# A decoder layer on one core: values ahead of the next scores, one scale on GpSimd, wider splits and sums, reciprocals in pieces

## The chip, the cores and the metric

The kernel runs on one core of a Trainium2 chip. The core has TensorE (PE, with its weight loads shown as PEld), VectorE (DVE), ScalarE (ACT), GpSimd (POOL) and SyncE (SP), which issues most of the transfers. The metric is the device time of one execution in microseconds. All times here are from the kernel's own runs and from one profiled execution of it.

## The reference

One decoder layer over 512 tokens of width 1024, all in float32: a sparse attention (NSA, 8 heads of 64, 2 key/value heads) and a gated linear attention (GLA, 4 heads) side by side, then a cross attention to 256 memory tokens and a gated feed-forward layer with a short convolution. Cut to what the change touches:

```python
for l in range(DEPTH):                                   # DEPTH = 1
    h = rms_norm(x, ln_mix_g)
    q_a, kv_a, gate_a, q_b, k_b, v_b, r_b, alpha_b, merge = split(h @ w_in)
    # NSA: for each block of queries three attentions (compressed, selected, window)
    #   s = q k - slope * distance; p = masked_softmax(s); o = p v
    #   out = gate0 * o_cmp + gate1 * o_slc + gate2 * o_win
    # GLA: b = cumsum(log_sigmoid(a_low @ w_alpha2 + b_alpha) / 16)  in chunks of 64 tokens
    #   q_d = q exp(b); k_d = k exp(-b); k_s = k exp(b_last - b)
    #   o = causal(q_d k_d^T) v + q_d state;  o = o * rsqrt(mean(o*o) + eps) * norm_g * silu(r)
    mix = sigmoid(m_nsa) * (o_nsa @ w_branch_nsa) + sigmoid(m_gla) * (o_gla @ w_branch_gla)
    x = x + mix @ w_out
    x = x + memory_cross_attention(rms_norm(x, ln_x_g), rms_norm(mem, ln_mem_g))
    x = x + conv_ffn(rms_norm(x, ln_ffn_g))              # (gelu(conv(u)) * g) @ w_down
return rms_norm(x, ln_final_g)
```

With 8 blocks of 64 tokens and 8 to select, the selected attention sees every earlier key.

## The kernel before

Activations are kept transposed, 128 features by 512 tokens a tile. Each float32 operand x of a product is split into h (rounded, by ACT) and l = x - h (by DVE), and a product is three matmuls: `mm3` (L160 to L162). Weights come in 141 blocks of 128x1024 from one array; `convert` (L140 on ACT, L141 on DVE) splits each block as it arrives. `split` (L165 ACT, L166 DVE) does the same for activations; it is a helper, so its instructions are told apart by their tiles.

The stages follow each other as proj, nsa, gla, mem/mix/mkv/wout, xat, xo, up/down. The NSA stage is a loop over 2 key/value heads (kv) and 4 query blocks of 128 tokens (i):

- `nsa_scores(kv, i)` makes scores for four heads g (L597 to L613 on PE), adds the position bias and takes maxima on DVE (L603, L615), scales the maxima (L622), takes exponentials with sums on ACT (L631), makes the coefficients on DVE (L634 reciprocal, L635), and multiplies the probabilities in place: the selected part `ss[g]` on DVE for g = 0, 1, 2 (L639) and on ACT for g = 3 (L641), the window part `sw[g]` on ACT for even g (L643) and on GpSimd for odd g (L645), the compressed part on GpSimd (L646). `ss` is 128x128(i+1), `sw` at most 128x384.
- `nsa_values(kv, i, ...)` transposes the probabilities of all four heads on PE (L669), splits them (tiles pth, ptl, pc), and accumulates the products with the values (L663) in one bank; then it adds two halves (L688) and splits the output into the tiles ON, two 128x128 pieces per block.
- between them, `fill` puts in work of the GLA projections ("fill" tiles: dense products of 24 matmuls, and `gla_decay` with its cumulative sums at L450).

The program states the operations in the order of the Python text. At build time each operation is put into the queue of its engine: of those that are then estimated to be ready, the one that stands earlier in the program goes first. Each engine runs its queue strictly in that fixed order. So matmuls of "fill" stand among those of the scores in the PE queue, and a later operation of the program stands behind an earlier one on its engine where both are ready.

Buffers are pools of equal tiles by tag: 43 of "g" (128x512), 16 of "s", 4 of "pair" (128x2x512). In `rsqrt` (L227, L228) ACT takes the root and DVE the reciprocal of the whole tile.

Of the kernel before, what the change touches and what calls it, by code (L numbers as in the profile page):

```python
# [10 lines left out]
F32R = mybir.dt.float32r  # L11
U32 = mybir.dt.uint32
AF = mybir.ActivationFunctionType
ALU = mybir.AluOpType
AX = mybir.AxisListType

P = 128
T = 512
# [17 lines left out]
def _layout(items):  # L36
# [14 lines left out]

CO, CO_COLS = _layout([
    ("ident", 128), ("ones", 128), ("slc", 512), ("win", 384), ("cmp", 124),
    ("chunk", 128), ("nslope", 24), ("slope", 8), ("qscale", 4), ("valid", 1), ("eps", 1),
])


# [1 line left out]
def layer_kernel(ctx: ExitStack, tc: tile.TileContext, xT, memT, W, small, const, gfin, out, out_t, order):  # L59
    nc = tc.nc  # L60
# [5 lines left out]
    def sb(shape, dtype, tag, bufs):  # L66
        uid[0] += 1
        return pool.tile(shape, dtype, name=f"{stage[0]}_{tag}_{uid[0]}", tag=tag, bufs=bufs)

    GB, SB, TB = 43, 16, 6  # L70

    def g_(dtype=F32):
        return sb([P, T], dtype, "g", GB)


    def pair():
        return sb([P, 2, T], F32R, "pair", 4)

    def s_(dtype=F32):
        return sb([P, T], dtype, "s", SB)  # L80
# [23 lines left out]
    def C(name):  # L104
        a, b = CO[name]
        return cst[:, a:b]
# [57 lines left out]
    def split(h, l, src):  # L164
        nc.scalar.activation(h, src, AF.Copy)  # L165
        nc.vector.tensor_sub(l, src, h.bitcast(F32))  # L166
# [58 lines left out]

    def rsqrt(dst, src, scale, refine=False):
        nc.scalar.activation(dst, src, AF.Sqrt, scale=scale, bias=C("eps"))  # L227
        nc.vector.reciprocal(dst, dst)  # L228
        if refine:
            v = sb([P, 4], F32, "newton", 2)[:, :dst.shape[-1]] if dst.shape[-1] <= 4 else t_()[:, :dst.shape[-1]]  # L230
            nc.vector.scalar_tensor_tensor(v, src, EPS / scale, dst, op0=ALU.add, op1=ALU.mult)
            nc.vector.scalar_tensor_tensor(v, v, -0.5 * scale, dst, op0=ALU.mult, op1=ALU.mult)
            nc.vector.scalar_tensor_tensor(dst, v, 1.5, dst, op0=ALU.add, op1=ALU.mult)
# [187 lines left out]
    def gla_decay():  # L421
        alT = bank("pt")
        for t in range(4):
            nc.tensor.transpose(alT[0:16, t * P:(t + 1) * P], alpha[t], C("ident"))
        als, wa = t_(F32R), sb([P, 256], F32R, "walpha", 1)
        nc.gpsimd.memset(als.bitcast(F32), 0.0)
        nc.gpsimd.memset(wa.bitcast(F32), 0.0)
        nc.scalar.activation(wa[0:16], S("walpha")[0:16], AF.Copy)
        nc.scalar.activation(wa[32:48], S("walpha")[0:16], AF.Copy)
        nc.vector.tensor_sub(wa[64:80], S("walpha")[0:16], wa[0:16].bitcast(F32))  # L430
        split(als[0:16], als[32:48], alT[0:16])
        nc.scalar.activation(als[64:80], alT[0:16], AF.Copy)
        zs = []
        az = sb([P, 2, T], F32, "raw", 3)
        for m in range(2):
            ps = bank("pt")
            nc.tensor.matmul(ps, wa[:, m * P:(m + 1) * P], als, start=True, stop=True)
            z = t_()
            nc.scalar.activation(z, ps, AF.Identity, bias=S("b_alpha")[:, m:m + 1])
            nc.scalar.activation(az[:, m], ps, AF.Abs, bias=S("b_alpha")[:, m:m + 1])  # L440
            zs.append(z)
        nc.scalar.activation(az, az, AF.Exp, scale=-1.0)
        nc.scalar.activation(az, az, AF.Ln, bias=1.0)
        for m in range(2):
            z = zs[m]
            nc.vector.scalar_tensor_tensor(z, z, 0.0, az[:, m], op0=ALU.min, op1=ALU.subtract)
            cs = g_()
            for c in range(8):
                v = slice(c * 64, c * 64 + 64)
                nc.vector.tensor_tensor_scan(cs[:, v], C("ones")[:, 0:64], z[:, v], 0.0, op0=ALU.mult, op1=ALU.add)  # L450
            cum[m] = cs


# [108 lines left out]
    fillers.append(gla_k(1))  # L562


    ON = [None] * 4

    def nsa_scores(kv, i):
        n = P * (i + 1)
# [66 lines left out]
        nc.vector.tensor_mul(cf, cf, gates[i][:, kv * 12:(kv + 1) * 12].rearrange("p (g b) -> p b g", b=3))  # L635
        for g in range(4):
            a, b = ss[g][:, :n], sw[g][:, :nw]
            if g < 3:
                nc.vector.tensor_scalar(a, a, cf[:, 1, g:g + 1], None, op0=ALU.mult)  # L639
            else:  # L640
                nc.scalar.activation(a, a, AF.Copy, scale=cf[:, 1, g:g + 1])  # L641
            if g % 2 == 0:
                nc.scalar.activation(b, b, AF.Copy, scale=cf[:, 2, g:g + 1])  # L643
            else:
                nc.gpsimd.tensor_scalar(b, b, cf[:, 2, g:g + 1], None, op0=ALU.mult)  # L645
# [2 lines left out]

    def nsa_values(kv, i, j0, ss, sw, cm):
        if i == 0:  # L650
            for a in range(2):
                ON[kv * 2 + a] = (g_(F32R), g_(F32R))
        qs = slice(i * P, (i + 1) * P)
        jobs = [([ss[g][:, kt * P:(kt + 1) * P] for g in range(4)], V2[kt][:, kv, :]) for kt in range(i + 1)]
        for kt in range(j0, i + 1):
            jobs.append(([sw[g][:, (kt - j0) * P:(kt - j0 + 1) * P] for g in range(4)], V2[kt][:, 2 + kv, :]))
        jobs.append(([cm[:, g] for g in range(4)], VC[:, kv, :]))
        po = bank("o")
        last = len(jobs) - 1

        def product(j, v, *parts):
            for x in parts:
                nc.tensor.matmul(po, v, x, start=j == 0 and x is parts[0], stop=j == last and x is parts[-1])  # L663

        ready = None
        for j, (srcs, v) in enumerate(jobs):
            pt = bank("pt")
            for g in range(4):
                nc.tensor.transpose(pt[:, g * P:(g + 1) * P], srcs[g], C("ident"))  # L669
            if j < last:  # L670
                h, l = sb([P, T], F32R, "pth", 2), sb([P, T], F32R, "ptl", 2)
                split(h, l, pt)
                parts = (h, l)
            else:
                x = PC[i % 2]
                split(x[0:32], x[32:64], pt[0:32])
                parts = (x,)
            if ready is not None:
                product(*ready)
            ready = (j, v) + parts  # L680
        product(*ready)
        bot = t_()
        nc.scalar.activation(bot[0:64], po[64:128], AF.Copy)
        of = t_()[:, 0:2 * P].rearrange("p (a q) -> p a q", a=2)
        pv = po.rearrange("p (a b q) -> p a b q", a=2, b=2)
        bv = bot.rearrange("p (a b q) -> p a b q", a=2, b=2)
        for b in range(2):
            nc.vector.tensor_add(of[b * 64:(b + 1) * 64], pv[0:64, :, b, :], bv[0:64, :, b, :])  # L688
        for a in range(2):
            h, l = ON[kv * 2 + a]  # L690
            split(h[:, qs], l[:, qs], of[:, a])

    stage[0] = "nsa"
    prev = None
    for kv in range(2):
        for i in range(4):
            cur = nsa_scores(kv, i)
            if prev is not None:
                nsa_values(*prev)
            prev = cur  # L700
            fill(NSA_FILL[kv * 4 + i])
    nsa_values(*prev)

# [201 lines left out]
    for n in range(0, 8, 2):  # L905
        th = [merge(C_MG, n, t_), merge(C_MG, n + 1, t_)]
        for j in range(2):
            ps = branch("w_branch_gla", OG, n + j)
            nc.vector.scalar_tensor_tensor(th[j], th[j], 1.0, ps, op0=ALU.add, op1=ALU.mult)
            nc.gpsimd.tensor_tensor(th[j], pm[n + j], th[j], op=ALU.add)  # L910
            if n < 4:
                x = pair()
                h, l = x[:, 0], x[:, 1]
            else:
                h, l = g_(F32R), g_(F32R)
            split(h, l, th[j])
            mix.append((h, l))

# [75 lines left out]
    def xat_values(hd, prs):  # L994
        po = bank("o")
        vs = slice(hd * P, (hd + 1) * P)
        for kt in range(2):
            pt = bank("pt")
            for i in range(4):
                c = (i % 2) * MEM + kt * P  # L1000
                nc.tensor.transpose(pt[:, i * P:(i + 1) * P], prs[i // 2][:, c:c + P], C("ident"))
            h, l = sb([P, T], F32R, "pth", 2), sb([P, T], F32R, "ptl", 2)
            split(h, l, pt)
            mm3(po, (XV[kt][0][:, vs], XV[kt][1][:, vs]), (h, l), kt == 0, kt == 1)
        h, l = g_(F32R), g_(F32R)
        split(h, l, po)
        xo[hd] = (h, l)

# [49 lines left out]
    def up(fs):  # L1058
# [14 lines left out]
        for f in fs:  # L1073
# [11 lines left out]
            gm = s_()  # L1085
            nc.vector.tensor_mul(gm, pg2, rstd)
            nc.gpsimd.tensor_tensor(gm, gm, cv, op=ALU.mult)  # L1087
            if f - fs[0] < 4:
                x = pair()
                h, l = x[:, 0], x[:, 1]  # L1090
            else:
                h, l = g_(F32R), g_(F32R)
            split(h, l, gm)
            act.append((h, l))
        return act
# [163 lines left out]
def _const(np):  # L1259
    z = np.zeros((P, CO_COLS), np.float32)  # L1260

    def put(name, a):
        a0, a1 = CO[name]
        z[:, a0:a1] = a
# [52 lines left out]
```

## Time and profile before

| what | value |
|---|---|
| median of 3 runs | 867.87 us (867.67 to 869.98) |
| profiled execution, its own time | 867.91 us |
| its span | 866.1 us, so 1.8 us lie around it |
| PE busy | 848.0 us, 98% of the span |
| DVE busy | 565.4 us, 65% |
| ACT busy | 425.6 us, 49% |
| POOL busy | 177.7 us, 21% |

In the rows, a group of instructions is named by line, engine, operation and tiles (out<-in), and a bracket at the end of a row of the timeline gives the engine's idle time before it and what ended that.

### The profile page before, as it was taken

How to read it: one execution, taken by the hardware profiler on the slowest of the kernel's cores; microseconds unless marked ns; L12 is line 12 of the kernel's file. 1: busy time of each engine (PE TensorE's matmuls, PEld its weight loads, DVE VectorE, ACT ScalarE, POOL GpSimd, SP SyncE). 2: the span in 40 equal slices, each digit the busy share in tenths (PEclk: the TensorE clock that was granted, in tenths of full speed). 3: DMA queues.
4: the chain of work that ended last, by engine and by line, in shares of the span. 5: the costliest groups of instructions: out<-in, count | busy, mean ns of one | idle time of the engine just before them, and what ended most of it. 6: DMA issues, size and time to landing. Idle time of an engine off the chain costs nothing.

```text
span 866.1 us, 11096 instructions
## 1 busy us (share of the span) xinstructions
PE 848.0 (98%) x4172; PEld 705.9 (81%) x4172; DVE 565.4 (65%) x923; ACT 425.6 (49%) x742; POOL 177.7 (21%) x157
## 2 busy tenths in 40 slices
PE   9999999999999999999999999999999999999997
PEld 6988767777887888898888888888888888888996
DVE  7576897998979576464487669666433456556324
ACT  7466868788544455354455535433311233334311
POOL 2373343331000023202200312111100121211121
PEclk9999999999999999999999999999999999999999
DMA  8332212002121242244341132222222222223302
GB/s 291 117 128 98 73 50 73 26 1 97 50 73 55 92 146 98 97 149 145 127 140 49 50 121 98 98 98 97 98 98 97 98 98 96 99 92 104 122 25 98
DMA packets 26407, 83.58 MB, mean 97 GB/s; under 512 B 3056, under 2 KB 5104, under 8 KB 26352
## 3 DMA queue, kind: packets, MB, share of 16 engines
q1 hardware_dynamic: 26064, 82.58, 28.1%
q8 instruction: 33, 0.54, 0.2%
q10 hardware_dynamic: 288, 0.28, 0.1%
q14 instruction: 22, 0.18, 0.1%
HBM read 80.76 MB, written 2.10 MB: 96 GB/s over the span
## 4 chain that ended last, share of the span: by engine, by line
PE 84%; DVE 7%; ACT 5%; issue 2%; POOL 1%; DVEq 0%; POOLq 0%; ACTq 0%
PE up_ps_sc L160 4%; PE up_ps_sc L161 4%; PE up_ps_sc L162 4%; PE fill_ps_acc L160 3%; PE up_ps_pt L160 3%; PE up_ps_pt L161 3%; PE up_ps_pt L162 3%; PE fill_ps_acc L161 3%; PE fill_ps_acc L162 3%; PE up_ps_acc L160 3%; PE up_ps_acc L161 3%; PE up_ps_acc L162 3%; ACT nsa_s L631 2%; PE down_ps_sc L162 2%; PE down_ps_sc L161 2%
## 5 line engine op out<-in xcount | busy, mean ns | idle before, releaser
L1087 POOL TENSOR_TENSOR up_s<-up_s,up_s 128x512 f32<-128x512 f32 x22 | 38.0, 1728 | 256.9 <-ACT up_wh L140 203.9
L140 ACT ACTIVATE up_wh<-up_raw 128x1024 fp32r<-128x1024 f32 x40 | 42.5, 1062 | 60.1 <-PE up_ps_sc L161 33.2
L141 DVE TENSOR_TENSOR up_wl<-up_raw,up_wh 128x1024 fp32r<-128x1024 f32 x40 | 61.6, 1541 | 15.5 <-ACT up_wh L140 15.3
L160 PE MATMUL up_ps_sc<-xo_g,up_wh 128*128 128x512 f32 x124 | 48.3, 389 | 0.0
L162 PE MATMUL up_ps_sc<-xo_g,up_wl 128*128 128x512 f32 x124 | 48.3, 389 | 0.0
L161 PE MATMUL up_ps_sc<-xo_g,up_wh 128*128 128x512 f32 x124 | 48.2, 389 | 0.0
L160 PE MATMUL up_ps_pt<-xo_g,up_wh 128*128 128x512 f32 x104 | 40.5, 389 | 0.0
L162 PE MATMUL up_ps_pt<-xo_g,up_wl 128*128 128x512 f32 x104 | 40.5, 389 | 0.0
L161 PE MATMUL up_ps_pt<-xo_g,up_wh 128*128 128x512 f32 x104 | 40.5, 389 | 0.0
L631 ACT ACTIVATE nsa_s<-nsa_s,nsa_nm 128x128 f32<-128x128 f32 (+3 forms) x64 | 34.2, 536 | 9.8 <-DVE nsa_nm L622 9.8
L160 PE MATMUL fill_ps_acc<-in_g,fill_wh 128*128 128x512 f32 x96 | 38.3, 399 | 0.2 <-DVE fill_t L548 0.2
L162 PE MATMUL fill_ps_acc<-in_g,fill_wl 128*128 128x512 f32 x96 | 38.1, 397 | 0.0
L161 PE MATMUL fill_ps_acc<-in_g,fill_wh 128*128 128x512 f32 x96 | 37.9, 395 | 0.0
L160 PE MATMUL up_ps_acc<-xo_g,up_wh 128*128 128x512 f32 x88 | 34.2, 389 | 0.0
L161 PE MATMUL up_ps_acc<-xo_g,up_wh 128*128 128x512 f32 x88 | 34.2, 389 | 0.0
L162 PE MATMUL up_ps_acc<-xo_g,up_wl 128*128 128x512 f32 x88 | 34.2, 389 | 0.0
L1083 ACT ACTIVATE up_s<-up_s 128x512 f32<-128x512 f32 x22 | 13.8, 632 | 40.6 <-DVE up_s L1081 40.6
L140 ACT ACTIVATE down_wh<-down_raw 128x1024 fp32r<-128x1024 f32 x9 | 9.5, 1061 | 39.4 <-PE down_ps_sc L161 17.5
L162 PEld LDWEIGHTS up_ps_sc<-xo_g,up_wl 128*128 128x128 f32 x124 | 23.3, 188 | 4.9
L160 PEld LDWEIGHTS up_ps_sc<-xo_g,up_wh 128*128 128x128 f32 x124 | 23.3, 188 | 4.8
L161 PEld LDWEIGHTS up_ps_sc<-xo_g,up_wh 128*128 128x128 f32 x124 | 23.3, 188 | 4.8
L165 ACT ACTIVATE nsa_pth<-nsa_ps_pt 128x512 fp32r<-128x512 f32 x38 | 21.8, 591 | 10.1 <-PE nsa_ps_pt L669 9.9
(975 smaller groups left out, 2687.4 us busy)
## 6 DMA issues: line engine op xcount, KB each, us to landing
up_raw<-in_w SPq DMA_DIRECT2D x44, 512.0 KB, 3.2
fill_raw<-in_w SPq DMA_DIRECT2D x20, 512.0 KB, 3.2
down_raw<-in_w SPq DMA_DIRECT2D x18, 512.0 KB, 3.3
proj_raw<-in_w SPq DMA_DIRECT2D x14, 512.0 KB, 3.8
mix_raw<-in_w SPq DMA_DIRECT2D x12, 512.0 KB, 3.2
mkv_raw<-in_w SPq DMA_DIRECT2D x8, 512.0 KB, 3.2
wout_raw<-in_w SPq DMA_DIRECT2D x8, 512.0 KB, 3.4
in_s<-in_xT SPq DMA_DIRECT2D x8, 256.0 KB, 5.5
```

The source lines that it names most:

```text
L140: nc.scalar.activation(wh[:, c], r[:, c], AF.Copy)
L141: lo.tensor_tensor(wl[:, c], r[:, c], wh[:, c].bitcast(F32), op=ALU.subtract)
L160: nc.tensor.matmul(ps, w[0], x[0], start=first, stop=False)
L161: nc.tensor.matmul(ps, w[0], x[1], start=False, stop=False)
L162: nc.tensor.matmul(ps, w[1], x[0], start=False, stop=last)
L165: nc.scalar.activation(h, src, AF.Copy)
L631: nc.scalar.activation(s[:, :w], s[:, :w], AF.Exp, scale=sl, bias=nm[:, c:c + 1], accum_out=sums[:, c:c + 1])
L1083: nc.scalar.activation(cv, cv, AF.Gelu_apprx_tanh)
L1087: nc.gpsimd.tensor_tensor(gm, gm, cv, op=ALU.mult)
```

## The change

1. In the loop of the NSA stage, the program states `nsa_values` of the block before ahead of `nsa_scores` of the block at hand, no longer behind it.
2. The selected part of head g = 1 is multiplied on GpSimd, ahead of the window part of that head, no longer on DVE.
3. The output tiles of NSA come two to a pair, and the split of a block's output is one operation on 128x2x128 on either engine, no longer two on 128x128.
4. The cumulative sums of the decay are one scan of 512 per tile, no longer eight of 64; a new constant "reset" (0 at the start of each 64, else 1) is multiplied in. The constants grow by 512 columns, 256 KB.
5. The reciprocal in `rsqrt` goes in pieces of at most 128 columns.
6. Buffers: "g" 43 to 35, "pair" 4 to 8, so split tiles of NSA's output, mix, cross attention and of 8 of the 11 activations of `up` come from pairs; a scratch for transfers shrinks from 4096 to 1024.

```diff
-    ("chunk", 128), ("nslope", 24), ("slope", 8), ("qscale", 4), ("valid", 1), ("eps", 1),
+    ("chunk", 128), ("nslope", 24), ("slope", 8), ("qscale", 4), ("valid", 1), ("eps", 1), ("reset", 512),
...
-    GB, SB, TB = 43, 16, 6
+    GB, SB, TB = 35, 16, 6
...
-        return sb([P, 2, T], F32R, "pair", 4)
+        return sb([P, 2, T], F32R, "pair", 8)
+
+    def pair_hl():
+        x = pair()
+        return x[:, 0], x[:, 1]
...
-        nc.vector.reciprocal(dst, dst)
+        n = dst.shape[-1]
+        for a in range(0, n, P):
+            nc.vector.reciprocal(dst[:, a:min(n, a + P)], dst[:, a:min(n, a + P)])
...
             cs = g_()
-            for c in range(8):
-                v = slice(c * 64, c * 64 + 64)
-                nc.vector.tensor_tensor_scan(cs[:, v], C("ones")[:, 0:64], z[:, v], 0.0, op0=ALU.mult, op1=ALU.add)
+            nc.vector.tensor_tensor_scan(cs, C("reset"), z, 0.0, op0=ALU.mult, op1=ALU.add)
...
-            if g < 3:
+            if g == 1:
+                nc.gpsimd.tensor_scalar(a, a, cf[:, 1, g:g + 1], None, op0=ALU.mult)
+            elif g < 3:
                 nc.vector.tensor_scalar(a, a, cf[:, 1, g:g + 1], None, op0=ALU.mult)
...
         if i == 0:
+            OX[kv] = (pair(), pair())
             for a in range(2):
-                ON[kv * 2 + a] = (g_(F32R), g_(F32R))
+                ON[kv * 2 + a] = tuple(x[:, a] for x in OX[kv])
...
-        for a in range(2):
-            h, l = ON[kv * 2 + a]
-            split(h[:, qs], l[:, qs], of[:, a])
+        split(*(x[:, :, qs] for x in OX[kv]), of)
...
         for i in range(4):
-            cur = nsa_scores(kv, i)
             if prev is not None:
                 nsa_values(*prev)
-            prev = cur
+            prev = nsa_scores(kv, i)
             fill(NSA_FILL[kv * 4 + i])
...
-            if f - fs[0] < 4:
-                x = pair()
-                h, l = x[:, 0], x[:, 1]
-            else:
-                h, l = g_(F32R), g_(F32R)
+            h, l = pair_hl() if f - fs[0] < 8 else (g_(F32R), g_(F32R))
...
+    put("reset", (np.arange(512)[None] % 64 > 0).astype(np.float32))
...
-    nc = _bacc.Bacc("TRN2", target_bir_lowering=False, num_devices=1, dynamic_dma_scratch_size=4096)
+    nc = _bacc.Bacc("TRN2", target_bir_lowering=False, num_devices=1, dynamic_dma_scratch_size=1024)
```

## Rows read from the trace of the kernel before

**Rows 1.** The page's first part: busy time of PE, share of the span, instructions.

```profile
PE 848.0 (98%) x4172; PEld 705.9 (81%) x4172; DVE 565.4 (65%) x923; ACT 425.6 (49%) x742; POOL 177.7 (21%) x157
```

**Rows 2.** Windows: stretch and its length, then busy time and instructions of PE, PEld, DVE, ACT, POOL, the granted clock, the DMA share and GB/s. NSA, two halves of GLA, and the end.

```profile
95.00:216.00 121.00, 114.28 (x592) 90.00 (x591) 106.36 (x285) 96.47 (x237) 42.78 (x49) 1.00 0.16 53
216.00:255.00 39.00, 38.94 (x205) 32.38 (x203) 30.70 (x58) 20.20 (x36) 0.00 (x0) 1.00 0.20 69
255.00:285.00 30.00, 27.67 (x146) 22.40 (x145) 28.02 (x45) 14.50 (x24) 1.05 (x2) 1.00 0.16 53
...
861.00:866.10 5.10, 0.00 (x0) 0.00 (x0) 0.91 (x3) 0.87 (x2) 0.00 (x0) 0.76 0.28 106
```

**Rows 3.** PE's waits from 95 to 216 us: who waited for whom, us in total, times, longest.

```profile
PE nsa_ps_o L663 <- DVE nsa_ptl L166: 3.6, 7, 1.1
PE nsa_ps_o L663 <- DVE nsa_t L688: 0.9, 2, 0.5
PE nsa_ps_sc L600 <- DVE nsa_mx L603: 0.6, 2, 0.4
...
PE nsa_ps_pt L669 <- DVE nsa_s L639: 0.3, 1, 0.3
```

**Rows 4.** The same from 216 to 300 us.

```profile
PE fill_ps_acc L160 <- DVE fill_g L718: 1.5, 1, 1.5
PE gla_ps_sc L765 <- ACT gla_t L165: 0.8, 1, 0.8
```

**Rows 5.** Timeline of DVE and PE, 118.6 to 121.6 us: start, duration, what (xcount merged).

```profile
118.67 1.77 DVE L639 TENSOR_SCALAR nsa_s<-nsa_s,nsa_cf 128x384 f32<-128x384 f32 x3
120.36 0.68 DVE L166 TENSOR_TENSOR nsa_ptl<-nsa_ps_pt,nsa_pth 128x512 fp32r<-128x512 f32 x1
...
121.09 0.50 PE L663 MATMUL nsa_ps_o<-nsa_ptl,proj_g 128*128 128x512 f32 x1 [1.11 <-DVE nsa_ptl L166]
```

**Rows 6.** Timeline of DVE, POOL, ACT and PE around 136 to 139 us.

```profile
136.19 1.88 DVE L639 TENSOR_SCALAR nsa_s<-nsa_s,nsa_cf 128x512 f32<-128x512 f32 x3
137.99 1.27 DVE L166 TENSOR_TENSOR nsa_ptl<-nsa_ps_pt,nsa_pth 128x512 fp32r<-128x512 f32 x2
...
136.31 2.86 POOL L645 TENSOR_SCALAR nsa_s<-nsa_s,nsa_cf 128x384 f32<-128x384 f32 x2 [5.72 <-ACT nsa_pth L165]
...
137.56 0.72 ACT L641 ACTIVATE nsa_s<-nsa_s,nsa_cf 128x512 f32<-128x512 f32 x1
...
138.72 0.50 PE L663 MATMUL nsa_ps_o<-nsa_ptl,proj_g 128*128 128x512 f32 x1 [0.38 <-DVE nsa_ptl L166]
```

**Rows 7.** Timeline of DVE and PE around 153 and 198 us.

```profile
152.53 0.84 DVE L639 TENSOR_SCALAR nsa_s<-nsa_s,nsa_cf 128x128 f32<-128x128 f32 x3
...
153.97 0.50 PE L663 MATMUL nsa_ps_o<-nsa_ptl,proj_g 128*128 128x512 f32 x1 [0.34 <-DVE nsa_ptl L166]
...
196.77 1.47 DVE L639 TENSOR_SCALAR nsa_s<-nsa_s,nsa_cf 128x512 f32<-128x512 f32 x2
...
198.89 0.50 PE L663 MATMUL nsa_ps_o<-nsa_ptl,proj_g 128*128 128x512 f32 x1 [0.56 <-DVE nsa_ptl L166]
```

**Rows 8.** Groups of DVE from 95 to 216 us, by form: busy us, mean ns of one | idle before.

```profile
L166 DVE TENSOR_TENSOR nsa_ptl<-nsa_ps_pt,nsa_pth 128x512 fp32r<-128x512 f32 x38 | 25.4, 681 | 0.9 <-ACT nsa_pth L165 0.8
L639 DVE TENSOR_SCALAR nsa_s<-nsa_s,nsa_cf 128x512 f32<-128x512 f32 x6 | 3.8, 681 | 0.1
L639 DVE TENSOR_SCALAR nsa_s<-nsa_s,nsa_cf 128x384 f32<-128x384 f32 x6 | 3.5, 642 | 0.0
L450 DVE TENSOR_TENSOR_SCAN fill_g<-in_cst,fill_t 128x64 f32<-128x64 f32 x16 | 3.0, 271 | 0.0
L639 DVE TENSOR_SCALAR nsa_s<-nsa_s,nsa_cf 128x256 f32<-128x256 f32 x6 | 2.5, 477 | 0.0
L639 DVE TENSOR_SCALAR nsa_s<-nsa_s,nsa_cf 128x128 f32<-128x128 f32 x3 | 0.8, 334 | 0.0
```

**Rows 9.** Groups of POOL from 95 to 215 us, by form.

```profile
L645 POOL TENSOR_SCALAR nsa_s<-nsa_s,nsa_cf 128x384 f32<-128x384 f32 x8 | 10.8, 1367 | 21.6 <-ACT nsa_pth L165 11.9 <-DVE nsa_cf L635 9.7
...
L645 POOL TENSOR_SCALAR nsa_s<-nsa_s,nsa_cf 128x128 f32<-128x128 f32 x2 | 1.3, 644 | 0.1
```

**Rows 10.** Timeline of DVE and POOL around 175 us: the two splits of one block's output, the second beside a POOL operation.

```profile
175.12 0.28 DVE L166 TENSOR_TENSOR nsa_g<-nsa_t,nsa_g 128x128 fp32r<-128x128 f32 x1
...
175.79 1.08 DVE L166 TENSOR_TENSOR nsa_g<-nsa_t,nsa_g 128x128 fp32r<-128x128 f32 x1
...
175.42 1.30 POOL L540 TENSOR_TENSOR fill_g<-fill_t,fill_t 128x512 f32<-128x512 f32 x1 [0.99 <-DVE nsa_g L166]
```

**Rows 11.** All reciprocals of L228 by tile (duration min/median/max in ns, first and last start), and a row of DVE's timeline.

```profile
L228 DVE RECIPROCAL gla_t<-gla_t x4: 3346/3350/3355, 253.9 to 308.0; 128x512 f32<-128x512 f32 x4
...
L228 DVE RECIPROCAL down_rstd<-down_rstd x1: 2553/2553/2553, 848.3 to 848.3; 128x384 f32<-128x384 f32 x1
...
276.27 0.69 DVE L718 TENSOR_TENSOR fill_g<-fill_ps_acc,proj_rstd 128x512 f32<-128x512 f32 x1
```

**Rows 12.** The start: the transfer of the constants (count, KB, us from issue to landing), ACT's conversion of the next weights, and PE's first matmul with them.

```profile
in_cst<-in_const SPq DMA_DIRECT2D x1, 721.0 KB, 6.5
...
18.59 2.35 ACT L140 ACTIVATE proj_wh<-in_raw 128x512 fp32r<-128x512 f32 x3
...
22.95 0.39 PE L160 MATMUL proj_ps_acc<-in_g,proj_wh 128*128 128x512 f32 x1
```

More of the change, by code (lines that the diff above doesn't have):

```diff
@@ L562, in layer_kernel @@
     fillers.append(gla_k(1))
-    ON = [None] * 4
+    ON, OX = [None] * 4, [None] * 2
     def nsa_scores(kv, i):
@@ L910, in layer_kernel @@
             nc.gpsimd.tensor_tensor(th[j], pm[n + j], th[j], op=ALU.add)
-            if n < 4:
-                x = pair()
-                h, l = x[:, 0], x[:, 1]
-            else:
-                h, l = g_(F32R), g_(F32R)
+            h, l = pair_hl()
             split(h, l, th[j])
@@ L1004, in xat_values @@
             mm3(po, (XV[kt][0][:, vs], XV[kt][1][:, vs]), (h, l), kt == 0, kt == 1)
-        h, l = g_(F32R), g_(F32R)
+        h, l = pair_hl()
         split(h, l, po)
@@ L1087, in up @@
             nc.gpsimd.tensor_tensor(gm, gm, cv, op=ALU.mult)
-            if f - fs[0] < 4:
[L1089 to L1092, printed above, removed]
+            h, l = pair_hl() if f - fs[0] < 8 else (g_(F32R), g_(F32R))
             split(h, l, gm)
```

## The prediction

> **What bounds the kernel now.** I read the page's first part, then windows by stage, then PE's waits, then the timelines around them. PE is busy 848.0 of 866.1 us [rows 1], so a change that removes no matmul can win back at most the 18.1 us in which PE rests, and of these 5.1 are the tail behind the last matmul [rows 2]. The windows tell where the rest lies: NSA (95 to 216 us) leaves PE idle 121.0 - 114.3 = 6.7 us, the second half of GLA (255 to 285) 2.3, the first half 0.1 [rows 2]. The granted clock is full in all three, so no clock is at stake. In NSA DVE is busy 106.4 of 121.0 us, 88%, against 65% over the whole span [rows 1, 2]: PE is the longest engine, but in this stage DVE runs nearly as long, and a queue that full answers late. PE's waits there say so: 3.6 us in 7 waits of the value product L663 for DVE's split of the transposed probabilities (nsa_ptl), 0.9 for L688, 0.6 for L603 [rows 3]. In GLA there are two waits, 1.5 for L718 on DVE and 0.8 for a split on ACT [rows 4].
>
> What DVE does ahead of the late split is the key reading. At 118.67 it runs three scales L639 in 1.77 us, then the split; PE waits 1.11 for it [rows 5]. At 136.19 three in 1.88 us, PE waits 0.38 [rows 6]; at 152.53 three in 0.84, PE waits 0.34; at 196.77 two in the window shown in 1.47, PE waits 0.56 [rows 7]. These scales belong to the next block's scores, stated earlier in the program than the values that wait. The four waits are 2.39 of the 3.6 us.
>
> **The change part by part.** The sum is made against the profiled execution's own 867.91 us, which is 0.04 above the median of the three runs.
>
> *Order and scale (parts 1, 2).* With the values stated first, a split that is ready stands ahead of the scales; so all four waits go: -2.39. A PE that resumes shows 0.50 us for its first product, where a nsa_ptl wait has just ended [rows 5 to 7], against 0.39 for a matmul in a running stream [rows 12]: 4 x 0.11 = 0.44 more. Together -2.8. If the new order gave nothing, one scale fewer would still shorten the queue by a third of each trio, 0.59, 0.63 and 0.28, and 0.73 at the fourth; capped by each wait that is 0.59 + 0.38 + 0.28 + 0.56 = 1.8. So -1.8 to -2.8; I take -2.8, since the splits were ready: in rows 5 and 6 the split starts as the last scale ends.
>
> What is late next in place of the split? The scales, behind up to two splits (1.27 us, rows 6), and with them the next block's transposes L669. Today L669 waits for L639 once, 0.3 us [rows 3]; matmuls of the fill work stand between in PE's queue and run on. The bounds are 0 and 8 blocks x 1.27 = 10.2; the nearest row is the 0.3, and I take two of these: +0.6.
>
> Nor does GpSimd delay the first product. Its row for 128x128 is 0.64 us and for 128x384 1.37 [rows 9], 0.36 per 128 columns, so 1.73 for 128x512, an estimate from these two. The first transposes of a block need all four heads, and ACT's scale for g = 3 ends at 137.56 + 0.72 = 138.28, that is 2.1 us after DVE began [rows 6]; GpSimd, which began at 136.31, would have ss[1] at 138.04. Behind it the two window scales end 1.73 later than now, 139.17 + 1.73 = 140.9. They are due after four jobs of the selected part, each four transposes and two products; at 0.9 us a job (an estimate: 0.50 for a product after a wait and 0.39 for the next, rows 6 and 12) that is 138.3 + 3.6 = 141.9. This cover of 1 us shrinks for shorter blocks: at i = 0, with one job ahead, it is 0.3 or so. I cost it at 0; without the cover it is up to 0.6 in each of the two short blocks. Queued behind on GpSimd are L646 and the GLA products, which in this stage leave GpSimd idle 121 - 42.8 = 78 us [rows 2].
>
> *DVE's load.* The dropped scale is 0.68, 0.64, 0.48 and 0.33 us by width [rows 8], 2.1 for a head and 4.3 for both, 3.9 where neighbours overlap. The output split was 0.28 twice [rows 10]; one of 256 columns costs about 0.42 (between 0.28 for 128 columns and 0.68 for 512, rows 8 and 10), so 0.14 x 8 = 1.1 less. The scans were 16 in 3.0 us, 0.27 each [rows 8]. For 512 columns the trace has none: if a scan costs like another operation of 512 columns it is 0.68, if nothing is won by width it is 3.0 / 2 = 1.5; 128 columns cost 0.28 and 512 0.68 elsewhere, so 0.15 is fixed, and (0.27 - 0.15) x 8 + 0.15 = 1.1. I take 1.1, nearest to the scan's own row: 0.8 saved, 0 to 1.6. In all DVE loses about 5.8 of 106.4 us, 5%. The three nsa_ptl waits that no scale explains (3.6 - 2.4 = 1.2 us) and the others on DVE (0.9 + 0.6 + the rest to 6.7, some 3 us) stand behind this queue. Bounds: 0, and all of the 4.2. I take two thirds of the first, -0.8, since splits also move forward, and 0.3 of the second, -0.9.
>
> *Contention between DVE and GpSimd.* The second output split at 175.79 took 1.08 us where the one before took 0.28; a GpSimd product that reads from SBUF ran from 175.42 to 176.72 [rows 10]. So a GpSimd operation can hold up DVE, and the change adds eight such. By the Trainium skill, "SBUF — State Buffer", section "Who interferes with whom", the two share one pair of ports as an exclusive lock for a whole instruction, whoever comes first; a DVE scale of one source would then wait for all of a GpSimd scale. In rows 6 three DVE scales finish in 1.88 us beside a GpSimd pair of 2.86 that began 0.12 after them; by the rule the second could not have begun before the first GpSimd scale ended at about 137.7. So the trace bears out the hold-up but not the whole lock, and the sum goes by the rows: two scales beside GpSimd cost what two of the three cost now. The strict reading is a rival below.
>
> *Reciprocals in pieces.* 512 columns take 3.35 us and 384 2.55 [rows 11]: 0.80 per 128, 0.15 fixed. Four pieces cost 4 x 0.95 = 3.8, or 3.5 where neighbours overlap by 0.09 as the splits do (2 x 0.68 against 1.27, rows 6 and 8): +0.2 to +0.5 each. Two lie ahead of the 1.5 us wait for L718 in GLA, at 253.9 and about 263; DVE is busy 28.0 of 30 us there [rows 2], so the price reaches PE: +0.4 to +1.0. Against this an operation that is ready may slip between pieces, at best the whole 1.5 back. I take +0.3. The other three (two of 512 and one of 384) lie where PE has other work: at 848.3 [rows 11], for example, matmuls run on until 861 [rows 2]. 0, at worst 0.5 each.
>
> *The start.* 256 KB more ride ahead of the weights: 721 KB land in 6.5 us beside other transfers, so 256 take at most 2.3. ACT takes the block behind them at 18.59 and is done with it and the next at 20.94; PE uses it at 22.95 [rows 12]. So 2.0 of the 2.3 are covered: 0, at worst +0.3. The buffers change places among pools with as many free as before: 0.
>
> Sum: -2.8 + 0.6 - 0.8 - 0.9 + 0.3 = -3.6, and 867.9 - 3.6 = 864.3 us.
>
> **The rivals.**
> - *More goes:* all of NSA's 6.7 us idle, and the 1.5 of GLA: 867.9 - 8.2 = 859.7. For it: most waits name DVE. Against it: ACT too is at 96.5 of 121.0 [rows 2], and a queue 83% full still answers late.
> - *Hidden:* DVE still has 100 of 121 us to do, the queues are dealt out anew, and other products wait instead: 867.9 - 1 = 866.9, within 2.6 either way. For it: three of the seven nsa_ptl waits, and all the others, have no trio of scales ahead. Against it: two thirds of the time of those seven has [rows 3, 5 to 7].
> - *Slower, the scores starve:* splits of the old block now delay maxima, exponentials and scales of the new one, a chain that is longer than a product. It decides if the fill work between runs out, that is if L669's wait grows from 0.3 once to over 0.45 in each of 8 blocks. At half of 1.27 per block it is 5.1, less the 2.8 won and with nothing of the rest: 867.9 + 2.3 = 870.2. For it: ACT, which makes the exponentials, is busy 96.5 of 121.0 us itself [rows 2], and can't catch up. Against it: in eight blocks PE waits for a scale once today [rows 3].
> - *Slower, the strict lock:* each of two DVE scales waits for a whole GpSimd scale, so at width 512 the pair ends after 1.73 + 0.68 + 1.37 + 0.68 = 4.5 us, not 1.3; 3.2 more, half of that in the mean block, 8 x 1.6 = 13 us of DVE. If half reaches PE, 867.9 - 3.6 + 6.4 = 870.7. This is the page's rule named above; the timeline of rows 6 speaks against it.
>
> **How the numbers follow.** Forecast 0.48 (own range 861.5 to 866), more goes 0.10, hidden 0.22, starving 0.15, strict lock 0.05. A measurement can tell about 0.3%, 2.6 us, from no change. Faster by more than that: 0.42 of the forecast, 0.10, and 0.03 of the hidden: 0.55. Slower: most of the last two, 0.19. Within: 0.26. The range 860.5 to 870.5 leaves out about 0.07 below and 0.08 above.
>
> **What would show it.** After the change no trio of scales stands between a finished transposition and its nsa_ptl split, and PE's waits at L663 for nsa_ptl fall from 3.6 to under 1.5 us. DVE's busy time in NSA falls by 5 to 6 us, with two L450 of about 1.1 us. L669's waits for the scales of DVE, ACT or GpSimd stay under 1 us; over 3 us there, the starving rival is right. DVE scales of 0.8 us and less refute the strict lock. PE idle between 95 and 285 us falls from 9.1 to about 5.5; if it is unchanged with other names at the waits, "hidden" is right. The prediction is wrong altogether if a stretch without change, before 95 or after 300 us, moves by more than 1 us.

## The result and the profile after

The changed kernel takes 875.12 us (median of 4 runs, 872.35 to 875.46) against 867.81 for the kernel before on the same chip: a ratio of 1.0073 [1.0057, 1.0088], 7.3 us slower. The forecast was 864.3, its range ended at 870.5. The profiled execution took 875.46 us, 1.8 of it around its span of 873.7. Executions more than 1.5% above the fastest of their kernel are left out of every median here; the profiled one of order_scan256 was such, so only its times are used.

The first part of the page, beside [rows 1]: PE is as busy as before (848.3 against 848.0 us). DVE lost 2.0 us in the whole, GpSimd gained 8.5.

```profile
PE 848.3 (97%) x4172; PEld 708.4 (81%) x4172; DVE 563.4 (64%) x913; ACT 423.2 (48%) x734; POOL 186.2 (21%) x165
```

Windows of the changed kernel, columns as in [rows 2]; the last runs from 95 us to a point in the next stage, its counterpart before follows.

```profile
95.00:216.00 121.00, 109.70 (x569) 87.93 (x568) 99.18 (x255) 93.06 (x226) 53.42 (x57) 0.99 0.13 44
216.00:255.00 39.00, 38.30 (x195) 31.55 (x195) 29.73 (x56) 18.73 (x33) 0.00 (x0) 1.00 0.23 82
255.00:285.00 30.00, 27.48 (x147) 22.45 (x146) 27.55 (x48) 15.65 (x24) 1.05 (x2) 0.99 0.10 36
95.00:317.00 222.00, 207.49 (x1057) 168.62 (x1056) 177.40 (x387) 140.82 (x303) 54.47 (x59) 0.98 0.17 59
```

```profile
95.00:310.00 215.00, 205.89 (x1054) 165.48 (x1053) 181.57 (x404) 141.91 (x311) 43.84 (x51) 1.00 0.18 61
```

Nearly the same work (1057 matmuls against 1054) takes 222 us in place of 215. PE rests 14.5 us there against 9.1, and its clock is 0.98 against 1.00: 5.4 of the 7.0 are rest and 1.6 longer busy time. DVE has 4.2 us less to do, and nothing of it arrived.

At 95 us the changed kernel is 1.0 us late already, by its first value product (before, then after); a wait at the start, for ACT's first conversion of weights, is new:

```profile
94.70 0.39 PE L663 MATMUL nsa_ps_o<-nsa_pth,proj_g 128*128 128x512 f32 x1
...
95.67 0.39 PE L670 MATMUL nsa_ps_o<-nsa_pth,proj_g 128*128 128x512 f32 x1
...
PE proj_ps_acc L164 <- ACT in_wh L144: 1.2, 1, 1.2
```

PE's waits, from 95 to 217 us and from 217 to 305 [rows 3, 4]:

```profile
PE nsa_ps_pt L676 <- POOL nsa_s L643: 5.5, 5, 1.7
PE nsa_ps_o L670 <- ACT nsa_pth L169: 2.9, 3, 1.7
PE fill_ps_acc L164 <- DVE fill_t L552: 1.1, 1, 1.1
PE nsa_ps_o L670 <- DVE nsa_ptl L170: 0.9, 1, 0.9
PE nsa_ps_pt L676 <- DVE nsa_s L645: 0.8, 2, 0.6
...
PE fill_ps_acc L164 <- DVE fill_g L722: 1.7, 1, 1.7
PE gla_ps_sc L769 <- ACT gla_t L169: 1.5, 2, 0.8
```

The waits for nsa_ptl fell from 3.6 to 0.9. Two others stand in their place: the transposes for GpSimd's scale (5.5 us; there was none) and the products for ACT's half of the split, nsa_pth (2.9; it was 0.4).

**The scale on GpSimd.** Timelines around 142 us: GpSimd, then DVE, ACT and PE (start, duration, what, and in brackets the idle time before it and what ended it).

```profile
142.34 1.29 POOL L544 TENSOR_TENSOR fill_g<-fill_t,fill_t 128x512 f32<-128x512 f32 x1 [0.26 <-ACT fill_t L540]
143.61 1.74 POOL L643 TENSOR_SCALAR nsa_s<-nsa_s,nsa_cf 128x512 f32<-128x512 f32 x1
145.33 2.85 POOL L651 TENSOR_SCALAR nsa_s<-nsa_s,nsa_cf 128x384 f32<-128x384 f32 x2
148.15 0.39 POOL L652 TENSOR_TENSOR proj_cm<-proj_cm,nsa_cf 128x124 f32<-128x124 f32 x1
148.50 1.28 POOL L543 TENSOR_TENSOR fill_g<-fill_t,fill_g 128x512 f32<-128x512 f32 x1
149.73 0.40 POOL L629 TENSOR_TENSOR proj_cm<-proj_cm,nsa_nm 128x124 f32<-128x124 f32 x1
...
142.36 2.38 DVE L645 TENSOR_SCALAR nsa_s<-nsa_s,nsa_cf 128x512 f32<-128x512 f32 x2
...
143.69 0.71 ACT L647 ACTIVATE nsa_s<-nsa_s,nsa_cf 128x512 f32<-128x512 f32 x1
...
143.97 0.33 PE L676 MATMUL nsa_ps_pt<-in_cst,nsa_s 128*128 128x128 f32 x1 [0.60 <-DVE nsa_s L645]
145.40 0.65 PE L676 MATMUL nsa_ps_pt<-in_cst,nsa_s 128*128 128x128 f32 x4 [1.10 <-POOL nsa_s L643]
```

The scale L643 takes 1.74 us, but stands behind a product of GLA (L544) and starts 1.25 us after DVE's. It is done at 145.35, 0.95 after ACT's scale for head 3 (144.40). PE transposes head 0 at 143.97 and has only head 1 next in its queue: 1.10 us of rest. At 174 us two such products stand ahead, and PE rests 1.73.

**And what stands behind it.** L629, the subtraction of the next block's maxima, ends GpSimd's queue in that stretch. ACT and PE after it:

```profile
150.16 0.31 ACT L630 ACTIVATE proj_cm<-proj_cm 128x124 f32<-128x124 f32 x1 [2.06 <-POOL proj_cm L629]
...
152.29 0.57 ACT L169 ACTIVATE nsa_pth<-nsa_ps_pt 128x512 fp32r<-128x512 f32 x1
...
152.92 0.50 PE L670 MATMUL nsa_ps_o<-nsa_pth,proj_g 128*128 128x512 f32 x1 [1.74 <-ACT nsa_pth L169]
```

ACT rests 2.06 us for L629, then does L630 and five exponentials in 2.1 us. The rounding L169, whose transposes had run at 150.58, stands behind them all in ACT's fixed queue, and PE behind it. ACT's group of L630 from 78 to 219 us sums this idle time (after the second bar), before and after the change:

```profile
L626 ACT ACTIVATE proj_cm<-proj_cm 128x124 f32<-128x124 f32 x8 | 2.4, 301 | 1.5 <-POOL proj_cm L625 1.5
```

```profile
L630 ACT ACTIVATE proj_cm<-proj_cm 128x124 f32<-128x124 f32 x8 | 2.4, 305 | 4.2 <-POOL proj_cm L629 4.2
```

**The clock.** Windows of the changed kernel around two of the rests:

```profile
117.00:120.40 3.40, 3.40 (x18) 2.51 (x16) 1.42 (x4) 3.38 (x11) 0.00 (x0) 1.00 0.09 35
120.40:123.70 3.30, 1.56 (x7) 1.00 (x6) 3.27 (x12) 3.30 (x8) 1.58 (x1) 1.00 0.00 0
123.70:127.10 3.40, 3.21 (x12) 2.92 (x13) 1.08 (x4) 1.62 (x4) 3.40 (x6) 0.50 0.00 0
...
281.40:283.20 1.80, 0.12 (x2) 0.08 (x1) 1.79 (x4) 1.78 (x2) 0.00 (x0) 1.00 0.00 0
284.10:287.50 3.40, 3.40 (x10) 2.67 (x9) 2.48 (x4) 1.52 (x4) 0.00 (x0) 0.51 0.59 176
287.50:291.00 3.50, 3.50 (x20) 2.96 (x20) 1.85 (x4) 0.72 (x1) 0.00 (x0) 0.99 0.36 129
```

After each rest a stretch of 3.4 us runs at half the clock (1.2 GHz), with 12 and 10 matmuls where full stretches hold 18 to 20. The kernel before has no such stretch between 95 and 860 us. Every run lists its mean granted clock, and it comes in steps: of 25 runs of the kernel before beside the first four experiments, 19 at 0.998 or 0.999 took 867.4 to 868.2 us, and six at 0.996 took 869.4 to 870.1. All four runs of the changed kernel stood at 0.995, the one of 872.35 us too, so the clock doesn't tell it from the others. From 0.998 to 0.996 the median rises by 1.9 us, so two stretches are some 3.7, an estimate from that step; how far later waits take it up isn't settled.

### The profile page after: what moved, and what is told of

Read it like the earlier page. It is cut to its first block, busy times and chain, and to the rows that moved or that the text cites. A ratio compares the mean times of both kernels' runs of the same rounds, so it can differ in the third digit from the quotient of the medians.

```text
span 873.7 us, 11078 instructions
## 1 busy us (share of the span) xinstructions
PE 848.3 (97%) x4172; PEld 708.4 (81%) x4172; DVE 563.4 (64%) x913; ACT 423.2 (48%) x734; POOL 186.2 (21%) x165
## 4 chain that ended last, share of the span: by engine, by line
PE 84%; ACT 6%; DVE 4%; POOL 3%; issue 1%; DMA 1%; DVEq 0%; ACTq 0%; POOLq 0%
PE up_ps_sc L166 4%; PE up_ps_sc L164 4%; PE up_ps_sc L165 4%; PE fill_ps_acc L164 3%; PE fill_ps_acc L165 3%; PE fill_ps_acc L166 3%; PE up_ps_pt L166 3%; PE up_ps_pt L164 3%; PE up_ps_pt L165 3%; PE up_ps_acc L166 2%; PE up_ps_acc L164 2%; PE up_ps_acc L165 2%; ACT nsa_s L635 2%; PE down_ps_sc L166 2%; PE down_ps_sc L164 2%; PE down_ps_sc L165 2%
## 5 line engine op out<-in xcount | busy, mean ns | idle before, releaser
L1087 POOL TENSOR_TENSOR up_s<-up_s,up_s 128x512 f32<-128x512 f32 x22 | 35.5, 1615 | 258.3 <-ACT up_wh L144 206.4
L676 PE MATMUL nsa_ps_pt<-in_cst,nsa_s 128*128 128x128 f32 x152 | 25.0, 282 | 6.4 <-POOL nsa_s L643 5.5
L676 PEld LDWEIGHTS nsa_ps_pt<-in_cst,nsa_s 128*128 128x128 f32 x152 | 19.2, 144 | 13.0 <-POOL nsa_s L643 6.7
L170 DVE TENSOR_TENSOR nsa_ptl<-nsa_ps_pt,nsa_pth 128x512 fp32r<-128x512 f32 x38 | 25.2, 685 | 6.5 <-ACT nsa_pth L169 6.1
L169 ACT ACTIVATE nsa_pth<-nsa_ps_pt 128x512 fp32r<-128x512 f32 x38 | 21.6, 591 | 14.4 <-PE nsa_ps_pt L676 14.2
```

## The experiments

Eighteen kernels ran, in five groups, each beside the kernel before on the same chip, to which its ratio is made. That kernel's medians in the five were 867.9 to 868.7 us, so less than 1 us between kernels of different groups tells nothing. In the table, "places" are the stretches in which an engine's built queue differs from that of the kernel before with the new order alone (tiles compared without their numbers, g and pair counted as one); "ACT idle" is the number behind POOL in the group row above, from one profiled execution; the last column is the median of the runs at a granted clock of 0.998 or more, and their count.

| kernel | places PE/DVE/ACT | median us | ratio to before | ACT idle | at full clock |
|---|---|---|---|---|---|
| before | 57/51/46 | 867.9 | 1 | 1.5 | 867.8 (19) |
| after | - | 875.12 | 1.0073 [1.0057, 1.0088] | 4.2 | none |
| a_scale_dve | - | 870.01 | 1.0027 [1.0015, 1.0039] | 4.3 | 868.7 (1) |
| a_order_old | - | 871.35 | 1.0037 [1.0021, 1.0054] | 4.7 | 870.1 (1) |
| b_order | 0 | 864.45 | 0.9974 [0.9957, 0.9991] | 0.2 | 864.3 (6) |
| b_pool | - | 869.34 | 1.0018 [1.0009, 1.0027] | 4.3 | 869.2 (7) |
| b_both | 51/48/41 | 873.46 | 1.0058 [1.0042, 1.0073] | 4.3 | none |
| b_order_recip | 9/20/9 | 866.22 | 0.9973 [0.9959, 0.9987] | 0.2 | 864.3 (1) |
| b_order_scan | 76/58/45 | 870.17 | 1.0022 [1.0012, 1.0031] | 3.6 | 869.9 (7) |
| b_order_split | 49/38/38 | 869.99 | 1.0014 [1.0004, 1.0024] | 2.2 | 868.8 (1) |
| order_buf | 10/5/2 | 864.38 | 0.9953 [0.9935, 0.9971] | 0.2 | 864.4 (3) |
| order_copy0 | 0/1/0 | 864.84 | 0.9957 [0.9941, 0.9974] | 0.2 | 865.0 (3) |
| order_copy | 47/43/41 | 866.51 | 0.9984 [0.9974, 0.9993] | 1.8 | 866.4 (8) |
| order_copy128 | 65/53/42 | 871.64 | 1.0036 [1.0024, 1.0047] | 4.8 | 870.2 (1) |
| order_scan256 | 52/48/44 | 869.48 | 1.0015 [1.0005, 1.0024] | not read | 869.5 (8) |
| order_k_dve | - | 865.36 | 0.9971 [0.9951, 0.9992] | 0.2 | 865.0 (3) |
| a_k_dve | - | 867.23 | 0.9990 [0.9981, 1.0000] | 0.4 | 866.1 (1) |
| a_k_scale_dve | - | 868.09 | 0.9991 [0.9980, 1.0003] | 0.6 | 866.7 (4) |
| after_copy | - | 872.69 | 1.0048 [1.0031, 1.0065] | 4.0 | 871.3 (1) |
| after_copy256 | - | 869.57 | 1.0013 [1.0003, 1.0022] | 1.6 | 868.5 (3) |

### Order and scale, each undone and each alone

a_scale_dve is the changed kernel with head 1's scale back on DVE, a_order_old the changed kernel with the old order; b_order and b_pool are the kernel before with the one or the other alone.

```diff
-            if g == 1:
-                nc.gpsimd.tensor_scalar(a, a, cf[:, 1, g:g + 1], None, op0=ALU.mult)
-            elif g < 3:
+            if g < 3:
```

```diff
+            cur = nsa_scores(kv, i)
             if prev is not None:
                 nsa_values(*prev)
-            prev = nsa_scores(kv, i)
+            prev = cur
```

> The changed kernel with head 1's selected scale back on DVE; all else as changed. Theory P (GpSimd's scale is late: it stands behind GLA products on GpSimd and is held up by DVE, and PE's transposes wait for it, 5.5 us in 5 waits): the waits of the transposes for GpSimd are gone, the time falls by 4 to 8 us to 867 to 871. Theory O (the order: values first let PE stand at transposes before the scales are made, whoever makes them): the transposes now wait for DVE or ACT as long, time 873 to 876. Theory R (the rest, scans, splits, pieces, constants): unchanged within 2 us of 875.

> The changed kernel with the old order of the program, scores ahead of the values of the block before; GpSimd's scale stays. Theory P: 872 to 876, the waits for GpSimd's scale stay at 3 us or more. Theory O: 864 to 869, the transposes wait under 1 us. Theory R: 873 to 876.

> The kernel before with the new order alone. Theory P: 863 to 868, the waits for nsa_ptl fall from 3.6 to under 1.5 us as forecast. Theory O: 871 to 876, with waits of the transposes of 4 us or more. Theory R: 867 to 869.

> The kernel before with head 1's selected scale on GpSimd alone. Theory P: 871 to 876, with waits of the transposes for GpSimd's scale of 3 us or more. Theory O: 865 to 869, those waits under 1 us. Theory R: 866 to 869.

The order alone gives 3.5 us. PE's waits in NSA with it:

```profile
PE nsa_ps_o L663 <- DVE nsa_ptl L166: 1.1, 2, 0.6
PE fill_ps_acc L160 <- DVE fill_t L548: 0.8, 1, 0.8
PE nsa_ps_pt L669 <- DVE nsa_s L639: 0.6, 3, 0.2
```

The scale alone costs 1.4, and 5.1 on top of all the rest. But the rest too costs: 870.0 with the order and without the scale, against 864.45.

Order and scale don't add up. With the old order, in a_order_old and b_pool, PE waits for no scale of GpSimd, where theory P told 3 us or more, and neither time, 871.4 and 869.3, lies in a range of any theory. Undoing the order in the changed kernel gains 3.8 us, though alone it is worth 3.5: with the values first the transposes reach GpSimd's scale before it is made. PE's longest waits in a_order_old are for ACT:

```profile
PE nsa_ps_o L670 <- ACT nsa_pth L169: 3.2, 2, 1.9
```

### What in the rest costs

b_both adds the scale to b_order; the next three add one of the other parts each (the scan with its constant and the smaller scratch, the split with the buffers).

```diff
+        for a in range(0, n, P):
+            nc.vector.reciprocal(dst[:, a:min(n, a + P)], dst[:, a:min(n, a + P)])
...
+            nc.vector.tensor_tensor_scan(cs, C("reset"), z, 0.0, op0=ALU.mult, op1=ALU.add)
...
+        split(*(x[:, :, qs] for x in OX[kv]), of)
```

> The kernel before with the new order and the scale on GpSimd, without the wide scans and splits, the pieces and the buffers. Theory P (a GpSimd scale that stands late on its engine costs whatever else changes; order + rest went from 870.0 to 875.1 us by it): 864.4 + 3 to 5 = 867.5 to 869.5, with waits of the transposes for GpSimd's scale of 3 us or more. Theory I (the scale is dear only together with the rest; alone on the kernel before it cost 1.4): 864.4 + 1.4 = 865.8 or less, such waits under 1.5 us.

> The kernel before with the new order and the reciprocals in pieces, nothing else. The rest (scans, splits, pieces, buffers) costs 5.6 us over the new order alone (870.0 against 864.4). If the pieces are its main part (four pieces of 0.9 us for 3.35, two of them ahead of waits in the GLA stage): 867 or more, and the loss lies after 216 us. If they are not: 864 to 865.5.

> The kernel before with the new order, one scan of 512 per tile with the constant, and the smaller scratch, nothing else. If one scan of 1.2 us in place of eight of 0.27 holds up DVE's queue in NSA: 867 or more, loss between 73 and 216 us. If it only takes 0.9 us off DVE: 863.5 to 865.

> The kernel before with the new order, the output split of 256 columns and the buffers (35 of g, 8 pairs), nothing else. If the wide split or the changed buffers are the main part of the rest's 5.6 us: 867 or more. If they only take work off DVE and ACT: 863 to 865. If none of the three reaches 867, the rest costs by its parts together, as other orders of the queues and half-clock stretches of PE after its longer idles, and not by one operation.

b_both took 873.5 us, 9.0 over the new order alone and far above both expectations; the sign of theory P is there:

```profile
PE nsa_ps_pt L671 <- POOL nsa_s L639: 3.8, 4, 1.6
```

At like clock the pieces cost nothing (864.3 as with the new order alone; 866.1 to 866.8 at 0.996 and 0.997, where that took 866.7). But six of the seven runs stood at the lower clock, and the median, 866.2, is 1.8 above and in neither range told. The scan costs 5.7 us and the split 5.5, each as much as both together with the pieces in a_scale_dve: these are no prices of single operations. The one scan is even 0.96 us shorter than eight of 0.27. What the costly ones share is the second column and the last but one: queues dealt out anew, and an ACT that waits for GpSimd. With the scan PE's first waits in NSA are:

```profile
PE nsa_ps_o L661 <- ACT nsa_pth L165: 2.3, 2, 1.5
PE nsa_ps_pt L667 <- DVE nsa_s L637: 2.2, 5, 1.0
```

### Other queues with the same work

One copy that nobody reads is added to b_order (with the smaller scratch, too): of 12 columns in block 0, 2 (order_copy) or, as a control told further on, in block 0, 0 (order_copy0), of 128 in block 0, 1 (order_copy128). order_buf takes the buffers without the wide split. a_k_dve attacks GpSimd's queue in the changed kernel.

```diff
+        if (kv, i) == (0, 2):
+            nc.vector.tensor_copy(sb([P, 3, 4], F32, "idle", 1), cf)
...
+        if (kv, i) == (0, 1):
+            nc.vector.tensor_copy(sb([P, P], F32, "idle", 1), ss[0][:, :P])
```

```diff
-            nc.gpsimd.tensor_tensor(k1, kf, k1, op=ALU.mult)
-            nc.gpsimd.tensor_tensor(k2, kf, e3, op=ALU.mult)
+            nc.vector.tensor_mul(k1, kf, k1)
+            nc.vector.tensor_mul(k2, kf, e3)
```

> The kernel before with the new order and one more instruction on DVE, a copy of 128x12 whose result nobody reads, in block kv = 0, i = 2 (at most 0.2 us of DVE). With it the planner deals the queues anew: 47 places on PE, 43 on DVE and 41 on ACT differ from the new order alone. Theory D (the draw of the queues, not the work of the scans and splits, is what costs): the time moves by 2 us or more from 864.4, most likely up, to 866.5 to 870, with new waits of PE for ACT's rounding nsa_pth or for the scales. Theory W (the work of the wide operations costs, by holding DVE): 864.0 to 864.8.

> The same as order_copy with a copy of 128x128 in block kv = 0, i = 1 in place of the one of 12 columns (at most 0.5 us of DVE); 65 places on PE and 53 on DVE differ from the new order alone. Theory D: another draw, anywhere from 863 to 870, and not the time of order_copy. Theory W: 864.0 to 865.

> The kernel before with the new order and the changed buffers alone: 35 of g, 8 pairs, NSA's output in pairs, but still two splits of 128 columns for each block; DVE and ACT do the same work as with the new order alone. Theory W for the wide split (its work or its later h is what took order + split + buffers from 864.4 to 870.0): 864 to 865. If the buffers cost: 868 to 870. Theory D, since PE's queue differs in 54 places, DVE's and ACT's in 27 and 25: 864 to 870.

> The changed kernel with the two products of GLA's keys that run on GpSimd (four of 1.30 us in NSA) on DVE. Theory P, with what stands ahead on GpSimd as its price: two of the five waits of the transposes for GpSimd's scale (1.10 and 1.73 us) stood behind such a product, and go; 875.1 - 2.8 = 872.3, or 870.5 if a half-clock stretch goes with them. If the price is the scale's own 1.2 to 2.0 us: the five waits stay, 874 to 877 with DVE's four more operations of 0.7 us.

The 54, 27 and 25 places told for order_buf counted tiles that only have another name; 10, 5 and 2 are real. It takes 864.4, so buffers are free. A copy of 0.2 us costs 7.2 us (order_copy128; 5.9 by its one run at full clock). Its waits in NSA, and the timeline of ACT and PE at the longest of them:

```profile
PE nsa_ps_o L665 <- ACT nsa_pth L165: 2.8, 2, 2.5
PE nsa_ps_pt L671 <- DVE nsa_s L641: 2.0, 7, 0.6
```

```profile
146.98 0.31 ACT L626 ACTIVATE proj_cm<-proj_cm 128x124 f32<-128x124 f32 x1 [3.98 <-POOL proj_cm L625]
...
148.35 0.80 PE L665 MATMUL nsa_ps_o<-nsa_pth,proj_g 128*128 128x512 f32 x1 [2.46 <-ACT nsa_pth L165]
```

It is the picture of the changed kernel, with no selected part on GpSimd: L625 stands behind the two window scales and a product of GLA. Theory D holds, though 871.6 lies above the 863 to 870 that it told; theory W, by which the work costs, is out for these.

a_k_dve comes out 5.1 us below its expectation. The wait at 174 us went and that at 144 fell from 1.10 to 0.53; the other three are 0.5, 0.8 and 1.0, after 0.5, 0.85 and 1.3. ACT's idle time fell from 4.2 to 0.4, and nsa_pth is no longer among the waits. PE's first wait, and ACT's group:

```profile
PE nsa_ps_pt L676 <- POOL nsa_s L643: 2.9, 4, 1.0
```

```profile
L630 ACT ACTIVATE proj_cm<-proj_cm 128x124 f32<-128x124 f32 x8 | 2.4, 300 | 0.4 <-POOL proj_cm L629 0.4
```

### Price or draw

a_k_scale_dve is a_k_dve with the scale on DVE; order_k_dve is order_buf with the key products on DVE; order_scan256 has each sum in two scans; after_copy and after_copy256 add an unread copy to the changed kernel (128x12 in block 0, 2; 128x256 in block 0, 1).

```diff
+            for c in range(0, 512, 256):
+                v = slice(c, c + 256)
+                nc.vector.tensor_tensor_scan(cs[:, v], C("reset")[:, v], z[:, v], 0.0, op0=ALU.mult, op1=ALU.add)
```

> The changed kernel with the two key products and head 1's scale on DVE, that is a_k_dve without the scale on GpSimd. Theory P (the scale on GpSimd has a price even with the products out of its way: 2.9 us of waits in a_k_dve): 867.2 - 2.9 = 864.3, at least 1.5 under a_k_dve. Theory D (the draw of the queues decides): anywhere from 864 to 871, also above a_k_dve.

> order_buf (new order and buffers, 864.4 us) with the key products on DVE. If the products hold up what else runs, by the port or on GpSimd: 862 to 864. If they only matter to a GpSimd scale behind them: 864.4 to 866 with DVE's 2.7 us more, or up to 870 with an unlucky draw.

> The new order with the unread copy of 128x12 in block kv = 0, i = 0, where the planner leaves every queue as it was (only this instruction is added). Theory D: 864.0 to 864.8, as the new order alone. If an added instruction costs by itself what order_copy showed: 866 or more.

> order_scan with each sum in two scans of 256 in place of one of 512. Theory W (the wide scan holds DVE for 1.2 us): about half of its 5.7 us over the new order alone, 866 to 868. Theory D (another draw: 52 places on PE differ from the new order alone): anywhere from 864 to 871; a time outside 866 to 868 speaks for it.

> The changed kernel and an unread copy of 128x12 on DVE in block kv = 0, i = 2; 48 places on PE, 11 on DVE and 6 on ACT differ from the changed kernel. If its 875.1 us are what its work costs: 874.8 to 875.6. Theory D: 2 us or more away from it; the waits of the transposes for GpSimd at 174 and 201 us change or go. Few places of ACT differ, so the smaller of the two moves.

> The changed kernel and an unread copy of 128x256 on DVE in block kv = 0, i = 1; 74 places on PE, 54 on DVE, 32 on ACT differ. If the 875.1 us are what its work costs: 875 to 876. Theory D: 866 to 875, likely below, since the draw of the changed kernel is the slowest of the ten seen so far.

The control holds: a copy that leaves the queues alone costs 0.4 us by the median and 0.7 at full clock (864.84, just over the 864.8 told). The narrower scans don't give half. The changed kernel with one copy more is 5.5 us faster (after_copy256) or 2.4 (after_copy), and theory P falls as a fixed price: with the key products off GpSimd the scale there costs nothing (ratio 0.9990 with it, 0.9991 without), though PE still waits 2.9 us for it. These two are one draw each as well.

Over the 17 kernels of the table with both numbers, ACT's idle time at L630 and the time at full clock go together: correlation 0.91, 1.2 us for each us; seven of the times are single runs. The column was read after the runs, so it is a finding about them and not a test passed. Clearing GpSimd's queue took both down in the two kernels that had something to clear (4.2 to 0.4 in a_k_dve; 4.3 to 0.6 from a_scale_dve to a_k_scale_dve); order_k_dve, at 0.2 from the start, gained nothing. No kernel moves L625 alone, so that its place is the cause, and not a sign of a bad draw, is argued and not shown.

## Why the prediction was wrong

- *The order, -2.8:* right alone. b_order has -3.5, nsa_ptl falls to 1.1 us, and L669's waits rise by 0.3 (forecast +0.6). Beside the scale on GpSimd it costs 3.8.
- *"I cost it at 0", the scale on GpSimd:* this step failed. Of the 10.8 us between forecast and time, 5.1 go when the scale goes back to DVE; the other 5.6 came with the rest (next point). The size was right (1.73 forecast, 1.74 at 142 us; 2.04 at 200 us). The cover was reckoned as if GpSimd began when DVE does; it began 1.25 us later, behind a product of GLA. And "queued behind on GpSimd are L646 and the GLA products" left out L625, the start of the next block's chain, on which ACT waits with all that stands behind it. GpSimd's 78 us of rest in the stage said nothing about either.
- *All terms together* took the queues as they are and summed edits to them. The copies show that the queues alone move the time by up to 7 us. "Hidden" named this and gave it 2.6 us either way, too little. That b_order's 864.45 meets the forecast of 864.3 for the whole is luck: it has one part of six.
- *DVE's load, -0.8 and -0.9:* the work went as forecast (scan 1.1 forecast, 1.20 measured; split 0.42, and 0.42; 4.2 us less DVE from 95 us on), the gain didn't follow. The rows, all instructions of a line, with min, median and max in ns:

```profile
L454 DVE TENSOR_TENSOR_SCAN fill_g<-in_cst,fill_t x2: 1194/1203/1212, 99.2 to 100.4; 128x512 f32<-128x512 f32 x2
L170 DVE TENSOR_TENSOR nsa_pair<-nsa_t,nsa_pair x8: 361/420/535, 106.2 to 219.1; 128x256 fp32r<-128x256 f32 x8
L234 DVE RECIPROCAL gla_t<-gla_t x16: 893/895/953, 259.7 to 318.0; 128x128 f32<-128x128 f32 x16
```

- *Contention, nothing beyond [rows 6]:* two thirds of the trio's 1.88 us are 1.25; the two scales at 142 us took 2.38, the first of them beside the product L544.
- *Pieces, +0.3:* near: 0.90 for 0.95 each, and the GLA wait grew from 1.5 to 1.7.
- *The start, 0:* the profiled execution has 1.2 us there. The constants aren't shown to be the cause: a_order_old has them and no such wait, b_order_split hasn't and waits 0.9. What brings it is open.
- *PE idle 95 to 285 us:* 14.5 for "about 5.5". *The stretches without change:* within the mark of 1 us, if barely: 1.0 late at 95 us, and 556.7 us from 317 on against 556.1 from 310.
- *Starving, 870.2, chance 0.15:* its sign and its mark came true (waits of the transposes for scales over 3 us: 6.3), its cause only in part: GpSimd's queue delays the scales, and not the splits, but with the old order (a_order_old) no wait for a GpSimd scale is left.
- *The clock:* "no clock is at stake" was read from a kernel with short rests. In the changed kernel half-clock stretches follow two of the longer rests.

## What to carry to other kernels

Before work goes to an engine with much idle time, read its queue at the very place: what stands ahead of the moved operation, and which first link of another engine's chain stands behind it. Where queues are dealt out at build time, an edit changes them all, so a part is priced only with a control that adds no work (an unread copy), several of them, and the time of one build is one draw. Here the order and the buffers alone, 864.4 us, beat both kernels; of the other parts, also with GpSimd's key products out of the way, no run shows a gain (867.2 us against 865.4).

## What was not expected of the hardware

GpSimd's products and its scales hold up DVE differently. The first of the two DVE scales at 142.36 took 1.55 us, the longest of all sixteen (median 0.45), and ended 0.28 after the product L544 did. In order_copy a DVE multiply of 12 columns, 0.17 us elsewhere, ran as long as the product beside it:

```profile
167.99 1.28 DVE L635 TENSOR_TENSOR nsa_cf<-nsa_cf,proj_gate 128x12 f32<-128x12 f32 x1
...
167.95 1.29 POOL L540 TENSOR_TENSOR fill_g<-fill_t,fill_t 128x512 f32<-128x512 f32 x1 [2.49 <-ACT fill_t L536]
```

Beside GpSimd's scale of one source (L643, 2.04 us from 200.12) DVE's scale at 201.21 took 0.49 and ended first; the second of the two at 142.36, beside L643 all its time, took 0.91 and ended 0.6 before it. So the whole lock of the Trainium skill ("SBUF — State Buffer", "Who interferes with whom"), which the prediction gave 0.05, agrees with the trace beside GpSimd's products of two sources and disagrees beside its scales, the only pair that [rows 6] shows; [rows 10] had shown the other.

After 1.74 us of rest between 120.4 and 123.7 us, and 1.68 before 283.1, the clock fell to half for 3.4 us, but not after each such rest: the 1.73 us at 174 us in the changed kernel brought none, nor did the 1.5 us in GLA before [rows 4]. Which rests do is left open.
